# Sixty counted increments replaced by a loop with a set head slot, with a 10 KB read on eight DMA engines ahead of it

## The chip, the cores and the metric

One core of one Trainium2 chip. The metric is the device time of one execution in microseconds (us), as the median of several runs. The profile's span, from the first to the last recorded instruction, is about 1.8 us shorter.

## The reference

```python
batch, m, k, n = 16, 512, 768, 1024          # float32
x: (batch, k, m)    y: (batch, k, n)
out = np.einsum('bkm,bkn->bmn', x, y)        # (batch, m, n)
```

Sixteen independent matrix products. x and y are 75.5 MB to read, out is 33.6 MB to write.

## The kernel before

SyncE (SP) issues every transfer on one queue. VectorE (DVE) casts x and y to bf16, TensorE (PE) multiplies, ScalarE (ACT) copies the sums out of PSUM. x and y have two buffers each, the output has five. Ahead of their real work DVE and ACT increment a semaphore `idle` sixty times; nobody waits for it. The increments put sixty more instructions ahead of the rest of each program.

```python
    def load(b):
        i = b % 2
        if b >= 2:
            nc.sync.wait_ge(cast, nx[b - 2])
        wide_dma("x", xs[i][:], x_v[b], 4, True).then_inc(sx[i], 16)
        if b >= 2:
            nc.sync.wait_ge(cast, nx[b - 2] + parts(b - 2))
        wide_dma("y", ys[i][:], y_v[b], 2, True).then_inc(sy[i], 16)
    # ... eight loads, five stores, four loads, four stores, four loads, the rest of the stores

    for _ in range(60):
        nc.vector.sem_inc(idle, 1)
    for b in range(B):
        # ... wait for x, cast it; wait for y, cast it (then_inc(cast, 1))

    # ... PE: a loop over the batches, 48 matmuls each

    nc.scalar.nop().then_inc(room, 2)
    for _ in range(60):
        nc.scalar.sem_inc(idle, 1)
    for b in range(B):
        if b >= NO:
            nc.scalar.wait_ge(so[b % NO], 16 * (b // NO))
        for g in range(2):
            nc.scalar.wait_ge(groups, 2 * b + g + 1)
            cp = nc.scalar.copy(ob[b % NO][...], ps[g][:])
            # ... then_inc(room, 1)
```

## Time and profile before

| | before |
|---|---|
| time, median of 4 runs | 260.71 us (260.67 to 260.78) |
| span of the profiled run | 259.0 us |
| DMA queue busy, share of 16 engines | 98.5% |
| bytes moved | 109.05 MB |
| instruction packets beside them (q14; "fetches" below) | 2, of 8,192 bytes and 0.309 us each |

The kernel is a copy with arithmetic beside it. The question for any change to it is which DMA engine finishes last. The prediction shows the views that say so; here is the one that shows the end itself: the last microseconds cut into windows. The columns are the window, its length, the busy time of PE, PE's weight loads, DVE, ACT and POOL with counts, the granted clock, the DMA share and GB/s. A packet counts in the window in which it starts.

```profile
255.00:256.00 1.00, 0.00 (x0) 0.00 (x0) 0.00 (x0) 0.00 (x0) 0.00 (x0) 0.50 1.00 426
256.00:256.50 0.50, 0.00 (x0) 0.00 (x0) 0.00 (x0) 0.00 (x0) 0.00 (x0) 0.50 0.16 66
256.50:257.00 0.50, 0.00 (x0) 0.00 (x0) 0.00 (x0) 0.00 (x0) 0.00 (x0) 0.50 0.16 66
257.00:257.50 0.50, 0.00 (x0) 0.00 (x0) 0.00 (x0) 0.00 (x0) 0.00 (x0) 0.50 0.08 33
```

A store packet of 16 KB takes 0.611 us, so one packet begun in a window of 0.5 us reads as 0.611 / (16 x 0.5) = 0.08. Fourteen of the sixteen engines have begun their last packet before 256.5 us; two go on, then one. That last one decides the time.

### The profile page before, as it was taken

To read this page: it belongs to the slowest core of one execution; us is meant where nothing else is said; L and a number is where in the kernel's file an instruction comes from. 1 tells how busy PE (TensorE), PEld (TensorE's weight loads), DVE (VectorE), ACT (ScalarE), POOL (GpSimd) and SP (SyncE) were. 2 spreads that over 40 slices of the span, in tenths; PEclk is the share of its full clock that TensorE was granted. 3 is DMA by queue.
4 is the path that set the end of the run, shared out by engine and by line. 5 is a ranking of instruction groups with operands and counts; after the bars stand their busy time and mean duration, and the time that the engine had idled before them with its cause. 6 is when DMAs were issued, how large, how long until landed. Compare 5 with 4: busy or idle time off the path is not lost. (4 is left out here: it accounts for less than half of the span.)

```text
span 259.0 us, 2506 instructions
## 1 busy us (share of the span) xinstructions
PE 179.0 (69%) x768; PEld 88.9 (34%) x768; DVE 82.0 (32%) x33; ACT 60.9 (24%) x33; POOL 0.2 (0%) x4
## 2 busy tenths in 40 slices
PE   0009999999999006999069999595008999969500
PEld 0004555554545002454025555252003555534200
DVE  0261645527164350002245263300242536410000
ACT  1000342244220005222202241433000234052300
POOL 0000000000000000000000000000000000000000
PEclk9999999999999855899759999999555999988965
DMA  7999989899999999999999998999999999999995
GB/s 270 428 490 395 471 380 478 380 471 395 456 402 448 387 428 425 433 463 456 410 440 410 440 448 377 435 423 463 471 387 471 395 456 410 395 428 438 423 435 240
DMA packets 4514, 109.07 MB, mean 421 GB/s; under 512 B 768, under 2 KB 768, under 8 KB 768
## 3 DMA queue, kind: packets, MB, share of 16 engines
q1 hardware_dynamic: 4512, 109.05, 98.5%
q14 instruction: 2, 0.02, 0.0%
HBM read 75.50 MB, written 33.55 MB: 421 GB/s over the span
## 5 line engine op out<-in xcount | busy, mean ns | idle before, releaser
L154 PE MATMUL ps<-yb,xb 128*128 x768 | 179.0, 397 | 64.3 <-PEq L149 64.3
L154 PEld LDWEIGHTS ps<-yb,xb 128*128 x768 | 88.9, 116 | 154.0 <-issue 82.6
L170 ACT COPY ob<-ps 128x2048 f32<-128x2048 f32 x32 | 59.6, 1872 | 179.0 <-PE ps L154 139.9
L132 DVE CAST yb<-ys 128x6144 bf16<-128x6144 f32 (+1 forms) x17 | 53.8, 3171 | 77.2 <-DMA ys<-in_y_dram 77.2
L128 DVE CAST xb<-xs 128x3072 bf16<-128x3072 f32 x16 | 28.2, 1760 | 68.3 <-DMA xs<-in_x_dram 53.7
L170 ACT ACT_TABLE_LOAD x1 | 1.3, 1283 | 5.3 <-issue 5.3
L200 POOL MEMSET const-bfloat16-1.0<- 128x1 bf16 x1 | 0.1, 103 | 0.0
L200 POOL MEMSET const-uint8-127<- 128x1 uint8 x1 | 0.1, 103 | 0.0
L200 POOL MEMSET const-float32-0.0<- 128x1 f32 x1 | 0.1, 99 | 0.2 <-issue 0.2
L200 POOL MEMSET const-float32-1.0<- 128x1 f32 x1 | 0.1, 99 | 0.0
## 6 DMA issues: line engine op xcount, KB each, us to landing
ys<-in_y_dram SPq DMA_DIRECT2D x16, 3072.0 KB, 18.6
out_dram<-ob SPq DMA_DIRECT2D x16, 2048.0 KB, 26.3
xs<-in_x_dram SPq DMA_DIRECT2D x16, 1536.0 KB, 20.1
```

The costliest lines, as they stand in the source:

```text
L128: nc.vector.tensor_copy(xb[:, i], xs[i][:]).then_inc(cast, 1)
L132: nc.vector.tensor_copy(yb[:, i, ks], ys[i][:, ks]).then_inc(cast, 1)
L154: mm = nc.tensor.matmul(ps[g][:, m, nt], x_w[:, bass.ds(s, 1), kt, mo], yb[:, bass.ds(s, 1), kt, nt * NF:(nt + 1) * NF], start=(kt == 0), ...
L170: cp = nc.scalar.copy(ob[b % NO][:, g * HB:(g + 1) * HB].rearrange("p m (t f) -> p m t f", f=NF), ps[g][:])
L200: nc = _bacc.Bacc("TRN2", target_bir_lowering=False, num_devices=1)
```

## The change

As I read it, its intent is that the place of the code no longer depends on a count of instructions. Each run of sixty increments becomes a loop of two passes with `head_slot` 0. ACT enters its loop only after an extra read has landed: eight rows of 10 KB of the first y, which is loaded in full right after anyway. The read goes to an output buffer that is not yet in use.

```diff
+    sw = ec(nc.semaphore("sw"))
...
         wide_dma("x", xs[i][:], x_v[b], 4, True).then_inc(sx[i], 16)
+        if b == 0:
+            nc.sync.dma_start(ob[0][0:32:4].rearrange("p m n -> p (m n)")[:, :2560],
+                              y_v[0, 0:32:4].rearrange("p k n -> p (k n)")[:, :2560]).then_inc(sw, 16)
...
-    for _ in range(60):
+    with nc.Fori(0, 2, engines=OrderedEngineSet([nc.vector.engine]), head_slot={nc.vector.engine: 0}):
         nc.vector.sem_inc(idle, 1)
...
     nc.scalar.nop().then_inc(room, 2)
-    for _ in range(60):
+    nc.scalar.wait_ge(sw, 16)
+    with nc.Fori(0, 2, engines=OrderedEngineSet([nc.scalar.engine]), head_slot={nc.scalar.engine: 0}):
         nc.scalar.sem_inc(idle, 1)
```

## The prediction

> **What bounds the kernel now.** I read the page's two DMA lines first, then the queue list, because a kernel that moves 109 MB in 259 us is suspect of being nothing but a copy.

> ```profile
> DMA  7999989899999999999999998999999999999995
> q1 hardware_dynamic: 4512, 109.05, 98.5%
> q14 instruction: 2, 0.02, 0.0%
> PE 179.0 (69%) x768; PEld 88.9 (34%) x768; DVE 82.0 (32%) x33; ACT 60.9 (24%) x33; POOL 0.2 (0%) x4
> ```

> The reader is to see that the sixteen DMA engines are busy in every slice but the first and the last, 98.5% of the span, and that no compute engine is above 69%. The stages by window say the same and show how little is left at the ends:

> ```profile
> 0.00:2.00 2.00, 0.00 (x0) 0.00 (x0) 0.00 (x0) 0.00 (x0) 0.20 (x4) 1.00 0.10 18
> 14.00:256.00 242.00, 178.96 (x768) 88.86 (x768) 80.23 (x32) 59.61 (x32) 0.00 (x0) 0.88 1.00 428
> 256.00:259.00 3.00, 0.00 (x0) 0.00 (x0) 0.00 (x0) 0.00 (x0) 0.00 (x0) 0.50 0.07 27
> ```

> The next to last column is the DMA share: 1.00 over 242 us. The chain that ended last names PE and ACT only (5% and 1%), and breaks off: it doesn't follow the queue. The bound is the transfers.

> With no idle time in the middle, the end is set by the one DMA engine that finishes last. No view gives that, so I took the transfer records out of the trace and strung them together: a packet belongs to the strand whose packet before it ended within 7 ns. Sixteen strands come out, nearly free of gaps; three records of some 4,500 do not fit. Each strand carries 6,815,936 bytes; the mean busy time is 255.1 us, the first packet starts at 1.97. Eight strands end their first packet at 2.7 to 3.3 us and eight at 3.4 to 3.6, a lead of 0.40 us for the first eight in the mean, which they keep. The strands end at 255.8 to 256.7, except two, at 257.72 and 257.54. These two, both of the early eight, are the ones with an instruction packet in them (the 2 of the q14 line; 8,192 bytes and 0.309 us each, at 8.95 and 10.96 us). In each the y packet after it took longer than the usual 0.912 us, by 0.25 and 0.55 us. So one fetch cost its strand 0.56 or 0.86 us, never made good. The first strand lost some 0.6 us more, mostly in 16 KB store packets of 634 to 645 ns instead of 611.

> What the two sequencers do at that time:

> ```profile
> 5.34 1.28 ACT L170 ACT_TABLE_LOAD   x1 [5.34 <-issue]
> 7.14 1.76 DVE L128 CAST xb<-xs 128x3072 bf16<-128x3072 f32 x1 [7.14 <-DMA xs<-in_x_dram]
> 15.05 3.36 DVE L132 CAST yb<-ys 128x6144 bf16<-128x6144 f32 x1 [6.14 <-DMA ys<-in_y_dram]
> 26.48 1.87 ACT L170 COPY ob<-ps 128x2048 f32<-128x2048 f32 x1 [19.86 <-PE ps L154]
> ```

> Behind the first line lie sixty semaphore increments on ACT, 0.067 us each, from 0.97 to 4.88, with one pause, 0.38 us before the last; sixty on DVE at 0.093 us end at 6.44. I read the pause as ACT passing into a new fetch block, and the two q14 packets as the fetches that ACT (at about 5 us) and DVE (at about 6.5) set off. That is inferred: the records don't name the engine that asked.

> [...]

> **The change part by part.**
> 1. Sixty increments become a loop of two passes on DVE and ACT. Removed: 60 x 0.093 = 5.6 us of DVE, 60 x 0.067 = 4.0 us of ACT. [...] None of it is on the path: DVE then waits for x0 until 7.14, and ACT's first copy waits for PE until 26.48. Direct worth: 0.
> 2. [...] I expect the same two blocks to be fetched, at other times. DVE enters at about 1.0 us, before the first data packet at 1.97, so its fetch can be served by an idle engine: its strand saves 0.56 to 0.86 us. If it meets the first x packets it costs at most the same again.
> 3. ACT first waits for the added read. That read follows x0 on each of the eight engines (x0 ends at 6.2 to 6.8 there; 10,240 bytes at 26.7 GB/s, the rate of a 12,288-byte packet in 0.460 us, are 0.38 us), so it lands at about 7.2 and ACT enters its block at 7.3 to 7.6 instead of 5.2. Its fetch then falls among the y packets, as before: 0.56 to 0.86 us on one strand. The table load of 1.28 us ends near 9 us, far ahead of 26.48.
> 4. The read adds 80 KB to 109.05 MB, but 0.38 us to each of eight strands. [...]this eats up their 0.40 us lead: the other strands would end by 256.9 instead of 256.7, which sets nothing as long as a strand with a fetch ends later. ACT's strand takes it in full.

> The sum, on the strand that ends last. Before: 257.72. After, ACT's strand, against the common end of 256.34: start -0.31 or -0.11, read +0.38, fetch +0.56 to +0.86, the slow stores 0 to +0.6. With middle values, -0.21 + 0.38 + 0.71 + 0.3 = +1.2, so 257.5; the extremes are near 257.0 and 258.1. That is -0.2 us, between -0.7 and +0.4. I lean to -0.3, since it takes only one strand in trouble instead of two, where the maximum of two counts. From 260.73 that gives 260.4 us.

> **The rivals.**
> - Both fetches leave the data stream, or ACT's is let in without the slow packet after it. Then a strand without a fetch sets the end, at 256.7 to 256.9: -0.8 to -1.0 us, 259.8. For it: the read was surely put there to time something. Against it: ACT's wait falls in the middle of the stream, which is full from 2 us on.
> - Both fetches stay at the old cost, or the jump to a block fetches 16 KB instead of 8, and the read adds its 0.38: +0.4 to +0.9, up to 261.6. [...]against it: the two single packets seen.
> - The fetch stalls DVE while its block comes in behind data (both packets waited some 4 us after their presumed trigger). A late first cast delays the third x load, but when that is issued at 8.93 the queue still holds y0, x1 and y1, up to 28 us. Hidden: 0.
> - Other phases between strands, so other store packets slow down: some tenths either way.

> **Range and chances.** No rival reaches 2%, which is 5.2 us: even a fetch doubled on the worst strand is under 1.5 us, and the floor under all of this, 16 full engines from 2 us on, lies about 1.5 us below the present end. The three times of before lie within 0.11 us, so noise is small. Predicted 260.4 us, range 259.8 to 261.1. Faster 0.01, within 2% 0.98, slower 0.01.

> **What would show it.** Step 1: DVE's first cast still at about 7.1 us. Step 2: an instruction packet near 1 to 2 us, or fewer than two among the data. Step 3: ACT's table load near 7.5 us and its fetch packet at some 9 to 12 us. Step 4: eight packets of 10,240 bytes, and the two groups of strands no longer 0.4 us apart. The strand with ACT's fetch should still end last. It would be wrong [...]if the fetch packets are more or other ones, or if DVE's first casts came so late that the load queue ran dry, which would show as DMA slices below 9 in the middle.

Where the texts speak of fetch blocks, units or boundaries, that is the reading of the q14 packets and of ACT's pause of 0.38 us; no trace shows where a block begins or ends.

## The result, and the profile after

The changed kernel takes 261.23 us (261.15 to 261.56, 4 runs) against 260.71: 0.52 us more. The ratio is 1.0022, interval 1.0005 to 1.0039. Here and below a ratio is the mean time of one kernel's runs over that of the other's in the same rounds, so not quite the ratio of the medians quoted. The change is within 2%, but above the range that was given, and on the other side of the time before.

The page of the changed kernel, the same four lines:

```profile
PE 176.0 (68%) x768; PEld 88.4 (34%) x768; DVE 82.0 (32%) x33; ACT 60.9 (23%) x33; POOL 0.2 (0%) x4
DMA  6999999898989999999999998999999999899995
q1 hardware_dynamic: 4528, 109.14, 98.3%
q14 instruction: 4, 0.03, 0.0%
```

Still a full queue, with no hole in the middle. The 16 packets more on q1 are the read: eight of 10,240 bytes, 0.385 us each, on eight strands, and eight of 4 bytes, 0.009 us each. The surprise is the last line: four instruction packets where before had two.

ACT and DVE at the start, from the timelines:

```profile
13.46 1.28 ACT L179 ACT_TABLE_LOAD   x1 [13.46 <-issue]
7.57 1.76 DVE L136 CAST xb<-xs 128x3072 bf16<-128x3072 f32 x1 [7.57 <-DMA xs<-in_x_dram]
15.99 3.36 DVE L140 CAST yb<-ys 128x6144 bf16<-128x6144 f32 x1 [6.65 <-DMA ys<-in_y_dram]
26.99 1.87 ACT L179 COPY ob<-ps 128x2048 f32<-128x2048 f32 x1 [12.25 <-PE ps L162]
```

The end of the span, in windows:

```profile
256.50:257.00 0.50, 0.00 (x0) 0.00 (x0) 0.00 (x0) 0.00 (x0) 0.00 (x0) 0.50 0.24 98
257.00:257.50 0.50, 0.00 (x0) 0.00 (x0) 0.00 (x0) 0.00 (x0) 0.00 (x0) 0.50 0.15 66
257.50:258.00 0.50, 0.00 (x0) 0.00 (x0) 0.00 (x0) 0.00 (x0) 0.00 (x0) 0.50 0.08 33
258.00:258.50 0.50, 0.00 (x0) 0.00 (x0) 0.00 (x0) 0.00 (x0) 0.00 (x0) 0.50 0.08 33
```

Three engines go on where two did, and the last starts its final packet in the window after 258 instead of the one after 257. Strung together, the transfer records give thirteen strands that end by 256.8 and three late ones: 258.00 (ACT's two late fetches), 258.64 (DVE's two) and 258.16, which has no fetch at all. The strand at 258.64 had one load packet that took 0.62 us longer than usual at 180 us, and this profiled run is the slowest of its four (261.56). The other three have spans of 259.4 to 259.5, which is where a last strand at 258.16 leads: from the last packet to the end of the span it was 1.26 us before.

The strand without a fetch lost its time elsewhere: its 128 store packets take 1.42 us more than 128 x 0.611. I call it **S**. The trace numbers no engine; S is known in each trace by its run of slow store packets, which only one strand at a time shows.

### The profile page after: what moved, and what is told of

Read it like the earlier page. It is cut to its first block, busy times and chain, and to the rows that moved or that the text cites. A ratio compares the mean times of both kernels' runs of the same rounds, so it can differ in the third digit from the quotient of the medians.

```text
span 259.8 us, 2403 instructions
## 1 busy us (share of the span) xinstructions
PE 176.0 (68%) x768; PEld 88.4 (34%) x768; DVE 82.0 (32%) x33; ACT 60.9 (23%) x33; POOL 0.2 (0%) x4
## 5 line engine op out<-in xcount | busy, mean ns | idle before, releaser
L162 PE MATMUL ps<-yb,xb 128*128 x768 | 176.0, 393 | 66.7 <-PEq L157 66.7
```

The costliest lines, as they stand in the source:

```text
L162: mm = nc.tensor.matmul(ps[g][:, m, nt], x_w[:, bass.ds(s, 1), kt, mo], yb[:, bass.ds(s, 1), kt, nt * NF:(nt + 1) * NF], start=(kt == 0), ...
```

## The experiments

All times are medians of five runs in five rounds, beside nine runs of the kernel before on the same chip. Their median is 260.74 for the first four kernels, 260.69 for the next six and 260.61 for the last two.

The first four take the change apart.

### e1: the read alone

The sixty increments stay; ACT waits for the read just before its first copy.

```diff
 # the kernel before
+        if b == 0:
+            (the same read of eight rows of 10 KB)
...
+        if b == 0:
+            nc.scalar.wait_ge(sw, 16)
         for g in range(2):
```

> The kernel before plus the added 80 KB read alone; ACT waits for it only at its first copy, so the sixty increments stay. Theory ([...]ACT and DVE fetch two units each, four instead of two; that is the main cost, and the read adds its 0.38 us to the strands that carry the fetches): two instruction packets as before, near 9 and 11 us; end about 0.3 to 0.4 us later than before, 261.0 to 261.1. Rival (the read is the whole cost, fetches cost the same wherever they fall): 261.2 to 261.3. Rival (the read only fills the lead of the early strands): 260.7.

Measured: 261.22 us (261.12 to 261.59), ratio 1.0022, interval 1.0008 to 1.0035. That is the cost of the whole change (0.52), within the noise. There are two instruction packets, at 8.68 and 10.56 us. The end, in windows:

```profile
257.00:257.50 0.50, 0.00 (x0) 0.00 (x0) 0.00 (x0) 0.00 (x0) 0.00 (x0) 0.50 0.08 33
257.50:258.00 0.50, 0.00 (x0) 0.00 (x0) 0.00 (x0) 0.00 (x0) 0.00 (x0) 0.50 0.08 33
258.00:258.50 0.50, 0.00 (x0) 0.00 (x0) 0.00 (x0) 0.00 (x0) 0.00 (x0) 0.50 0.00 0
```

S can be followed here from start to end. The two strands with a fetch end at 257.30 and 257.83. The last, at 258.18, is one of the eight that read, has no fetch, and lost 1.57 us in its store packets: S again. Packet by packet against S of before, it ends its x0 packets 0.07 us earlier, then carries the read (0.39 with its semaphore), loses 0.12 more in stores and 0.02 elsewhere: 0.46 in all, which takes 257.72 to 258.18. The theory, that the additional fetches are the main cost, falls with this run.

### e2: the loops alone

```diff
 # the changed kernel
-        if b == 0:
-            (the read)
-    nc.scalar.wait_ge(sw, 16)
```

> The changed kernel without the read and without ACT's wait for it. Theory: four instruction packets; both jumps at about 1 us, so both target units come in near 2 us beside the first x packets, and both following units near 8 us among y; time between before and the change, about 260.6 to 261.0. Rival (the read is the whole cost): as before, 260.7. Rival (the wait and ACT's late start are the cost): 260.7 or less.

Measured: 260.81 us (260.66 to 260.92), ratio 1.0003, interval 0.9989 to 1.0017: the time of before, with four instruction packets (2.02, 2.76, 7.71, 8.94 us):

```profile
q14 instruction: 4, 0.03, 0.1%
```

The strands that fetch end by 257.5, the last one at 257.7, where before ended too. Two fetches more cost nothing that can be told from the noise.

### e3: loop heads on slot 128

```diff
 # the changed kernel
-head_slot={nc.vector.engine: 0}      -head_slot={nc.scalar.engine: 0}
+head_slot={nc.vector.engine: 128}    +head_slot={nc.scalar.engine: 128}
```

> The changed kernel with both loop heads on slot 128 instead of slot 0, the read and the wait kept. Theory[...]: no 3 us stall of DVE at the jump and no 5 us stall of ACT, two instruction packets instead of four, DVE's near 2 us; time 260.2 to 260.9. Rival (any taken branch has its target fetched): four packets and the stalls as in the change, 261.2.[...]

Measured: 261.17 us (261.06 to 261.25), ratio 1.0015, interval 1.0002 to 1.0029. The page and ACT's timeline:

```profile
q14 instruction: 2, 0.02, 0.0%
9.17 1.28 ACT L179 ACT_TABLE_LOAD   x1 [9.17 <-issue]
```

Packets and stalls are as expected: two packets (4.15 and 12.29 us), DVE's branch takes 0.5 us instead of 3.1, and ACT's table load follows at 9.17 instead of 13.46. Why slot 128 comes with fewer packets and shorter branches than slot 0 is not shown. But the time stays that of the change, outside what I expected. S ends at 258.13 with half the fetches.

### e4: no increments at all

```diff
 # the kernel before
-    for _ in range(60):
-        nc.vector.sem_inc(idle, 1)
...
-    for _ in range(60):
-        nc.scalar.sem_inc(idle, 1)
```

> The kernel before without the sixty increments on either engine, no loop, no read. Theory (some fifty instructions follow on each engine, fewer than sixty, so no boundary is passed before the end): no instruction packet among the data, or one only near the end; no strand is late by a fetch, and the end comes 0.5 to 1.0 us earlier, 259.7 to 260.2. Rival (the boundary is passed somewhere in the middle, or the fetch costs the same at any time): two packets late in the span, 260.7.

Measured: 261.10 us (261.08 to 261.16), ratio 1.0014, interval 1.0000 to 1.0027: slower by 0.36, a miss in time. The profile is the most telling of all:

```profile
span 258.9 us, 2386 instructions
256.50:257.00 0.50, 0.00 (x0) 0.00 (x0) 0.00 (x0) 0.00 (x0) 0.00 (x0) 0.50 0.01 0
257.00:257.50 0.50, 0.00 (x0) 0.00 (x0) 0.00 (x0) 0.00 (x0) 0.00 (x0) 0.50 0.08 33
```

There is no q14 line on this page: not one instruction packet lies in the span. Every strand ends by 256.88 but one, which ends at 257.67, where before ended with its two fetches (257.72). Its store packets take 622 ns in the mean instead of 611, 1.45 us more in all; many of them are slow while PE and ACT work, hardly any after 243 us, about when the last copy is made. So S sets the end here, and in before no fetch did. The 0.36 us that this kernel loses lies outside the span: time less span is 2.2 us here, 1.8 us before. Its cause is not shown, since the records don't reach so far.

### What S costs: e5 to e12

The new theory: S, one of the eight engines that read, ends last, and pays for every byte that it is given. The rivals: a shift of eight strands against the other eight, or the extra transfer as such. Seven kernels change only the size or the number of engines of the read in e1; e8 goes back to the loops.

### e5: one row

```diff
 # e1
-  ob[0][0:32:4] ... [:, :2560]   <-   y_v[0, 0:32:4] ... [:, :2560]
+  ob[0][0:1] ... [:, :2557]      <-   y_v[0, 0:1] ... [:, :2557]
```

> The kernel before plus a read of one row of 2,557 elements (10 KB) on a single DMA engine instead of eight rows on eight. Theory now: one strand, S,[...] loses 1.5 us in its store packets in every run and ends last; the read costs only because S carries it, fetches end before S. If S is the engine that a one-row transfer uses, the time is that of the read on eight, 261.1 to 261.3; if it is another, 260.7. Rival (the read costs because it shifts eight strands against the other eight, or because x0 lands later): 260.7 in any case.

Measured: 260.69 us (260.55 to 260.81), ratio 1.0001, interval 0.9988 to 1.0015. One row of 10 KB is free; the last strand ends at 257.73, as before. If S pays for what it carries, it did not carry this row. By itself this run does not tell the theory from its rival.

### e6: 16 KB instead of 10

```diff
 # e1
-[:, :2560]
+[:, :4096]
```

> The kernel before plus a read of 16 KB instead of 10 KB[...]. Theory (S carries it byte for byte, at 26.7 GB/s 0.23 us more than 10 KB): 261.4 to 261.5, S ending 0.6 to 0.7 us later than before. Rival (a fixed cost of one more transfer, or of the shift): 261.2. Rival (early strands have room for some): nonlinear, more than 261.5.

Measured: 261.33 us (261.21 to 261.37), ratio 1.0026, interval 1.0012 to 1.0039: 0.64 us more than before, where the bytes alone are 0.61 (estimated at the 26.7 GB/s of a 12,288-byte packet in 0.460 us). S ends at 258.26; a strand with a fetch, at 258.31, has drawn level with it.

### e7: all sixteen engines

```diff
 # e1
-  0:32:4  (eight rows)
+  0:128:8 (sixteen rows)
```

> The kernel before plus a read of 10 KB on all sixteen engines. Theory (only S counts): the same as on eight, 261.1 to 261.3, though every strand ends some 0.4 us later than before. Rival (the shift of eight against eight costs): 260.9 to 261.1, only the bytes being paid. Rival (total bytes count): twice the cost, 261.7.

Measured: 261.67 us (261.47 to 261.77), ratio 1.0037, interval 1.0024 to 1.0051: 0.98 us more, a miss; it fits the rival of total bytes. The records give another reason. On eight of the strands, S among them, the first y packet after the read took about 0.46 us longer than its 0.912; the other eight lost 0.46 to 0.53 us over the read and that packet together. No such packet is in e1. With the read's 0.38 that is 0.84 us on S, which ends at 258.74, 1.0 later than before. Why those packets are late is not shown: e9 reads the first four of these rows, and no reader's first y packet there is over 0.09 us late.

### e8: the loops on slot 128, without the read

```diff
 # e2
-head_slot 0 on both engines
+head_slot 128 on both engines
```

> The changed kernel without the read and the wait, loop heads on slot 128. Theory (S ends last whatever the fetches do): two instruction packets, both at 2 to 5 us, and the time of before, 260.6 to 260.8. Rival (fetches set the end, as the prediction had it): 259.9 to 260.4.

Measured: 260.65 us (260.57 to 260.73), ratio 1.0000, interval 0.9986 to 1.0013. Both fetches come early (3.62 and 4.05 us); the last strand ends at 257.68. This is the change's intent without its cost: no count of instructions, and the time of before. It doesn't beat it.

### e9 and e10: four engines, two engines

```diff
 # e1
-  0:32:4   (eight rows)
+  0:32:8   (e9, four rows)      0:32:16  (e10, two rows)
```

> The kernel before plus the 10 KB read on four DMA engines (four rows). Theory (one strand, S, with slow store packets ends last in every run; the read costs only where S carries it): either the whole cost, 261.1 to 261.3 with S among the four that read, or none, 260.6 to 260.8 with S not among them; never between. Rival (the shift of the reading strands against the others costs, in proportion to their number): half the cost, 260.9 to 261.0.

> The same on two DMA engines. Theory: the whole cost if S is the second engine[...], else none, 260.6 to 260.8. Rival (cost in proportion to the number of shifted strands): 260.8 to 260.9.

Which strand the second row of e10 falls to was not known beforehand; that S could be only the second was the assumption.

Measured: 261.19 us for four (260.77 to 261.26; ratio 1.0013, interval 1.0000 to 1.0027) and 261.02 us for two (260.66 to 261.22; 1.0011, interval 0.9998 to 1.0025). These are inconclusive in time, and they spoil the plain form of the theory, which said all or nothing. The single runs of e9 lie at the time before (260.77, 260.86) or near that of e1 (261.19 to 261.26); those of e10 are spread over 260.66 to 261.22. In the profiled runs the last strand is S again, at 258.16 and 258.06. Where the reads begin, several strands run within 40 ns of each other, but neighbours on one strand nearly all overlap by 3 to 4 ns, and strung by that and by the order of the transfers S can be followed (in e10 past one exact tie at 92.7 us, which its slow stores decide): it read in neither. It was late all the same. Its first y packet took 1.087 and 1.059 us instead of 0.912, and it ended y0 at 13.99 and 13.94 against 13.71 before. So S here pays 0.2 to 0.3 us for reads that other strands carry; why is open.

### e11 and e12: 512 bytes, 32 KB

```diff
 # e1
-[:, :2560]                       # one read of 10 KB on each of eight
+[:, :128]                        # e11: 512 bytes
+[:, :4096], twice                # e12: two reads of 16 KB, into ob[0] and ob[1]; ACT waits for 32
```

> The kernel before plus a read of 512 bytes[...]: one more transfer, nearly no bytes. Theory (S,[...] pays for the bytes it carries, 0.02 us here): 260.7, within 0.1 of before. Rival (a fixed cost of one more transfer ahead of y0): 261.0 to 261.2, most of what 10 KB cost.

> The kernel before plus two reads of 16 KB each[...]. Theory (bytes on S at 26.7 GB/s, 32,768 bytes are 1.23 us): 1.2 to 1.4 us more than before, 261.9 to 262.1. Rival (a fixed cost per transfer): two times that of one 16 KB read's fixed part, below 261.7. Rival (total bytes over sixteen engines, 256 KB are 0.61 us): 261.3.

Measured: 260.62 us (260.52 to 260.84) with 512 bytes, ratio 1.0002, interval 0.9988 to 1.0015; 261.90 us (261.76 to 261.95) with 32 KB, ratio 1.0047, interval 1.0034 to 1.0061. The theory held in both; with 32 KB S ends at 258.83. The four sizes on eight engines side by side, each one's own time estimated at 26.7 GB/s, the rate of a 12,288-byte packet in 0.460 us:

| read on each of eight engines | its own time, estimated | cost in the median |
|---|---|---|
| 512 bytes (e11) | 0.02 us | 0.01 us |
| 10 KB (e1) | 0.38 us | 0.48 us |
| 16 KB (e6) | 0.61 us | 0.64 us |
| 32 KB (e12) | 1.23 us | 1.29 us |

An extra transfer on eight engines costs nothing as such that the noise would show. With eight readers the end moves by the bytes per engine, from 10 KB on: there is no slack in the last strand.

The strands that could be told apart, with the store time over 128 x 0.611 us of the one that I call S:

| kernel | instruction packets | strands with a fetch end | S ends | lost by S in stores |
|---|---|---|---|---|
| e4 (neither loops nor read) | 0 | none | 257.67 | 1.45 us |
| e1 (read) | 2 | 257.30, 257.83 | 258.18 | 1.57 us |
| e3 (read, slot 128) | 2 | 257.34, 257.56 | 258.13 | 1.56 us |
| the change | 4 | 258.00, 258.64 | 258.16 | 1.42 us |

## Why the prediction was wrong

- **What bounds the kernel** was right: the transfers, and of them the DMA engine that finishes last. The queue stays full in every kernel.
- **The step that failed** is the reading of which strand that is: "These two, both of the early eight, are the ones with an instruction packet in them", and the sum built "on the strand that ends last. Before: 257.72. After, ACT's strand". The strand at 257.72 has no fetch. Two strands, the one with the fetch at 8.95 us and the one with slow store packets, end a packet in the same nanosecond at 117.1 us, and my stringing swapped them there. Position alone can't tell them apart; the slow packets, which run on without a break on one strand, can, and the strand with that fetch ends at 256.5. The fetch and the slow stores were put down to one strand. The sign was there: 0.6 us "mostly in 16 KB store packets of 634 to 645 ns" did not fit a strand whose trouble was a fetch. e4 shows it: no fetch, and the same end. In the change's own profile ACT's strand, which the forecast had last, ends at 258.00, before S (258.16) and DVE's strand (258.64).
- **Step 4, the read**, was sized right: 0.38 us to each of eight strands, 0.385 measured. Its place in the sum was wrong: it was set against a fetch that would be cheaper, while the strand that ends last pays the read in full and gains nothing. Added to S of before, 257.72 + 0.38 is 258.10; S was at 258.13 to 258.18 in the three kernels with this read. The prediction's extremes had let the slow stores be a chance matter (0 to 0.6 us); on S they are 1.4 to 1.6 us, in every trace.
- **Step 2, the same two fetches at other times**, was wrong: there are four packets, of 8,192 bytes each. The rival of 16 KB allowed for more fetching, and I set it behind. Its +0.4 to +0.9 us takes in the measured +0.52, but by luck as far as the fetches go: the read's 0.38 in it is right, while e2 shows that two more fetches cost 0.07, inside the noise, since the strands with a fetch still end before S.
- **Step 1, no direct worth**, held: DVE's first cast moved from 7.14 to 7.57 and the queue did not run dry. **Step 3** was wrong in time: ACT's table load came at 13.46, not near 7.5. ACT's branch ran at 7.77 and its loop began at 12.96, as I read it because the branch waited for its target. That was hidden, as the step said of its delay.
- That the early eight are the eight that read, as step 4 took it, was right: the readers end x0 at 6.2 to 6.5 us, all but DVE's strand (6.8), and the others at 6.7 to 7.2.
- The gain of "one strand in trouble instead of two", which turned a sum near zero into a gain of 0.3 us, had nothing under it: the maximum was over another strand.

What stays open: which engine S is, why its stores are slow (622 to 623 ns in the mean for 16 KB, the others' 611, in every trace, on the three chips 9, 1 and 6 of e1 to e12), and why its store loss varies (1.45 us in before and in e4, 1.57 in e1, 1.42 in the change), which is as large as the 0.1 us that 10 KB cost beyond its bytes. e9 and e10 don't fit a strand that pays only for its own bytes: two or four readers cost about 0.3 us in the mean, with wide scatter, and S was not among them.

## What to carry to other kernels

In this kernel, whose DMA queue never empties, the time was that of the slowest DMA engine, and bytes put on it cost their full transfer time (0.48, 0.64 and 1.29 us for 0.38, 0.61 and 1.23) however well the read seemed hidden. Where a queue is as full, find that engine before placing filler transfers, and check by a variant in which the suspected cause is absent (e4), since strands that pass each other can be confused. Removing dead instructions cost 0.36 us outside the span (e4), so compare whole times, not spans alone. If a loop head is set on a slot by hand, try another slot too: slot 128 instead of slot 0 took DVE's branch from 3.1 to 0.5 us and ACT's from 5.2 to 0.4 (e3), though none of it showed in the time.
